# A planned two-layer decoder kernel: other durations in the planner, a time per change of TensorE's tile form, and the last sum in full width

## The chip, the core and the metric

The kernel runs on one core of one Trainium2 chip. The time is the device time of one execution in microseconds (us); lower is better. Three executions of the kernel before gave 816.85, 816.95 and 820.06 us, a median of 816.95. One execution was also recorded by the profiler; its views are what the prediction reads.

The core has five engines that run side by side, each through its own queue in order: TensorE (PE; its weight loads are PEld), VectorE (DVE), ScalarE (ACT), GpSimd (POOL) and SyncE (SP), which here only issues DMAs.

## What is computed

Two layers over 256 tokens of width 1024. Each layer mixes tokens by two attentions (nsa and moba) in parallel, merges them by gates, and then runs a gated feed-forward. In fp32 throughout:

```python
for l in range(DEPTH):                       # DEPTH = 2
    ada = jax.nn.silu(c) @ w_ada[l] + b_ada[l]
    sh_m, sc_m, g_m, sh_f, sc_f, g_f = jnp.split(ada[:, None, :], 6, axis=-1)
    h = rms_norm(x, norm_mix[l]) * (1.0 + sc_m) + sh_m
    ... = jnp.split(h @ w_in[l], split_at, axis=-1)
    y_a = nsa_mixer(...)     # compressed, selected and windowed attention
    y_b = moba_mixer(...)    # block attention
    gate_a, gate_b = jnp.split(jax.nn.sigmoid(g_br), 2, axis=-1)
    merged = gate_a * (y_a @ w_up_nsa[l]) + gate_b * (y_b @ w_up_moba[l])
    x = x + g_m * (merged @ w_out[l])
    h = rms_norm(x, norm_ffn[l]) * (1.0 + sc_f) + sh_f
    gt, up = jnp.split(h @ w_ffn_in[l], 2, axis=-1)
    x = x + g_f * ((jax.nn.silu(gt) * up) @ w_ffn_out[l])
return x
```

## The kernel before

**Tiling.** The 256 tokens are two tiles of 128 (t = 0, 1). Most weight matrices arrive in units of 128 x 2048 numbers (1 MB). A unit is split into a high part (`hi`, ScalarE, rounded to fp32r) and a low part (`lo`, VectorE, the rest), and a product is three matmuls of 512 columns: high by high, high by low, low by high (`mm3`). A few units are multiplied whole in fp32 instead (`raw`), where a matmul shows as two instructions of the trace. The split activations are called `hp` (the normalised input of a sublayer), `mT` (the merged attention) and `aT` (the feed-forward's inner tile); `yy` holds the attention outputs, which are multiplied whole.

**Stages of a run.** First a lead: constants, the first input and the first eight weight units. Then for each layer the attention (projections, score bursts `bank<-kk,qq`, softmax, value bursts `bank<-pt,vsw` and `bank<-pt,ve`, in which matmuls use 64 rows or 64 columns of the array), the up projections (`yy`), the output projection (`mT`), the joint to the feed-forward (residual sum, norm, transposes, scale and shift in `h_chain_`), the feed-forward in two halves, and a joint to the next layer.

**The planner.** The program isn't issued in the order in which it is written down. `Engines` (lines 561 to 680) records each operation as an `Op` with a duration for every engine that may run it, its predecessors, and the buffers it takes. `Program.order` (line 266) then simulates the engines with these durations: for each engine it looks at the operations that could start first, and among those within a small window (0.08 us for PE, 0.05 for DVE and ACT) takes the one of highest rank. The rank is the longest path to the end plus a boost; operations under `R.ahead()` rank above others on every engine but PE. `free[e]` is the time from which an engine may take its next operation, `ends` the time at which a result is there, and `LAT` what another engine waits beyond it. Where several engines may run an operation, the one that ends first takes it, with a handicap (`BIAS`). If PE would stand idle for long, `fill` puts dummy matmuls there (`bank<-zb`).

`Program.rounds` (line 532) makes 60 such plans. Each is replayed 8 times by `replay` (line 480) with its order held and random pauses in the DMAs; operations on chains that left PE waiting get a higher boost in the next plan. The plan whose replays ended soonest on average is emitted. The order of each engine's queue, of SP's too, is thus fixed ahead of the run; buffer waits and data waits are semaphores.

**Tile forms before.** An `Op` has a flag `parts`, true when a matmul uses fewer than 128 rows or columns. Only `replay` charges 0.1 us (`SWITCH[2]`) when the flag changes; `order` charges nothing.

**The last sum.** In the last layer's output product (line 1647 on) the four accumulators are (t, c), c being a half of the 1024 columns. For the last one, (1, 1), the last three weight units are added in two halves of 256 columns, each with its own residual sum (`resid`, line 1635) and output DMA:

```python
            parts[(NT - 1, 1)] = [(0, 256), (256, 512)]
            keys += [(i, t, k, c, e) for t in range(NT) for c in range(2) for e in parts[(t, c)]
                     for i in range(nu - nl, nu) for k in range(2)]
```

Of the kernel before, what the change touches and what calls it, by code (L numbers as in the profile page):

```python
# [107 lines left out]
def AP(x):  # L108
    return x.ap() if isinstance(x, Ref) else x
# [9 lines left out]
class Op:  # L119
    def __init__(self, no, alts, key):  # L120
# [5 lines left out]
        self.func, self.loads, self.parts, self.paced, self.then = None, None, False, False, None  # L126
# [5 lines left out]
FIRST = 1000.0  # L132
LAT = {"PE": 0.24, "DVE": 0.09, "ACT": 0.09, "POOL": 0.2, "SP": 0.0, "Q": 0.0}
# [5 lines left out]
class Program:  # L139
# [9 lines left out]
    SWITCH = (0.0, 0.0, 0.1)  # L149
# [116 lines left out]
    def order(self):  # L266
# [24 lines left out]
        parts = False  # L291
# [43 lines left out]
        while left:  # L335
# [6 lines left out]
            for op in ready:  # L342
# [15 lines left out]
            for e, cs in per.items():  # L358
# [3 lines left out]
                else:  # L362
                    w = eps[e] + (self.SWITCH[1] if e == "PE" else 0.0)
                    pick = max((c for c in cs if c[0] <= t0 + w), key=lambda c: (c[1].rank(e), -c[1].no))
# [38 lines left out]
            if e == "PE":  # L403
                parts = op.parts
# [14 lines left out]
            else:  # L419
                free[e] = t + c  # L420
# [21 lines left out]

    def fill(self, t0, t1):
# [15 lines left out]
        op.stage = "fill"  # L459
# [20 lines left out]
    def replay(self, steps, seed):  # L480
# [4 lines left out]
        dma, table, parts, gaps = 0.0, (), False, []  # L485
        for i, (e, op, c, deps) in enumerate(steps):
# [22 lines left out]
            free[e] = t + c  # L509
# [49 lines left out]
class Engines:  # L559
# [25 lines left out]
    def stt(self, out, a, s, b, op0, op1, accum=None):  # L585
# [5 lines left out]
                  [a, s, b], [out] + list(kw.values()), extra=0.08 if kw else 0.0)  # L591

    def ttr(self, out, a, b, op0, op1, init, accum):
        self._vec(("DVE",), cols(out), True,
                  lambda v: v.tensor_tensor_reduce(AP(out), AP(a), AP(b), 1.0, init, op0, op1, AP(accum)),  # L595
                  [a, b], [out, accum], extra=0.08)

    def ts(self, out, a, s1, s2, op0, op1=None, engs=("DVE",)):
# [3 lines left out]
                  [a, s1, s2], [out], psum=self._psum(a))  # L602
# [12 lines left out]
    def act(self, out, a, func, scale=None, bias=None, accum=None, late=()):  # L615
# [27 lines left out]
    def mm(self, out, lhsT, rhs, start, stop, cost=None):  # L643
# [6 lines left out]
        op.parts = AP(lhsT).shape[0] < P or AP(out).shape[0] < P  # L650

    def term(self, out, lhsT, rhs, first):
# [13 lines left out]
        self.p.op({"PE": (cost, [go])}, [lhsT, rhs], [out], term=s)  # L666

    def tr(self, out, a, ident):
        self.p.op({"PE": (0.109, [lambda: self.nc.tensor.transpose(AP(out), AP(a), AP(ident))])}, [a, ident], [out])  # L669
# [16 lines left out]

HALVED = 1
# [15 lines left out]
def trunk_kernel(tc, pools, A):  # L703
# [510 lines left out]
    def sublayer_mix(l, h):  # L1214
# [4 lines left out]
        ev, kv_, qv, vv, yv = (R.val(x_) for x_ in ("e", "kk", "qq", "ve", "yy"))  # L1219
# [7 lines left out]
        def whole_piece(d, src):  # L1227
            evac(d, src)
            return [(None, None, d[:, j * P:(j + 1) * P]) for j in range(4)]
# [571 lines left out]
```

## Time and profile before

| | us |
|---|---|
| median of three executions | 816.95 |
| the three executions | 816.85, 816.95, 820.06 |
| span of the profiled execution (first to last instruction) | 815.4 |

The executions shown are at least 1.45 us longer than the profiled span: the time around the first and the last instruction is not in the span.

How to read the lines that follow in the prediction. A line of the first view gives an engine's busy time, its share of the span and its instructions; in a line by stage, the bounds of the stage come first, then its length, the busy time of PE with the number of its instructions, the granted clock, the share of the DMA engines and GB/s. In a timeline a line starts with the time of start and the duration of the group (both in us), engine, line of the kernel, operation, result<-operands by the program's names, rows*columns for matmuls, the shape, and the number of instructions merged; in brackets stands how long the engine was idle before and what released it. In a list by form, two numbers after the bar are the busy time and the mean duration in ns. A line of one source line gives the least, the median and the greatest duration in ns. In the chain a line is start, length and what it was. L662 is the line of matmuls into shared sums, L648 that of other matmuls, L669 of transposes, L583 of VectorE's two-operand operations, L631 of ScalarE's.

### The profile page before, as it was taken

The page shows a single profiled execution, that of the slowest core. Times are in us where ns is not written, and L with a number is a line of the kernel's source. Part 1 is how long each engine was busy: PE and PEld are TensorE (multiplying, and loading weights), DVE is VectorE, ACT ScalarE, POOL GpSimd, SP SyncE. Part 2 cuts the span into 40 slices and gives each one's busy share as a digit, 9 for nine tenths or more (in the row PEclk, how much of TensorE's full clock was granted, in tenths as well). Part 3 has the DMA queues.
Part 4 walks back from the last instruction along what each step waited for, and adds up shares of the span by engine and source line. Part 5 has one row for each costly group of instructions (what it writes and reads, how often), then busy time and mean ns, then how long its engine had stood idle before and what let it go on. Part 6 is the DMA issues. An engine that isn't in the chain of part 4 may idle for free.

```text
span 815.4 us, 10543 instructions
## 1 busy us (share of the span) xinstructions
PE 803.8 (99%) x3997; PEld 610.0 (75%) x3997; DVE 580.2 (71%) x1025; ACT 410.3 (50%) x654; POOL 79.5 (10%) x75
## 2 busy tenths in 40 slices
PE   8999999999999999999999999999999999999997
PEld 4567656764878888888878887676477888889886
DVE  6889977677986877777788898776377526545454
ACT  5445366662673534433585566587347524433441
POOL 4702620000100000000000442000000000000000
PEclk9999999999999999999999999999999999999999
DMA  9967585538949887977855785540391645555441
GB/s 357 416 230 290 161 295 182 175 130 310 372 152 338 311 305 288 327 293 259 311 174 214 278 289 180 188 151 25 104 344 69 210 153 174 202 192 207 151 158 52
DMA packets 74018, 183.82 MB, mean 225 GB/s; under 512 B 4304, under 2 KB 9696, under 8 KB 73456
## 3 DMA queue, kind: packets, MB, share of 16 engines
q1 hardware_dynamic: 73920, 183.08, 63.0%
q8 instruction: 31, 0.51, 0.2%
q14 instruction: 19, 0.16, 0.1%
q0 software_dynamic: 48, 0.08, 0.0%
HBM read 182.10 MB, written 1.05 MB: 225 GB/s over the span
## 4 chain that ended last, share of the span: by engine, by line
PE 88%; DVE 4%; DMA 2%; ACT 2%; POOL 2%; issue 1%; SPq 0%; DVEq 0%; POOLq 0%
PE bank L662 77%; PE bank L648 6%; PE bank L669 5%; DMA rows<-in_rows 1%; DVE tmp L583 1%; DMA raw<-in_w_out 1%; DVE lo L583 1%; POOL tmp L601 1%; DVE tmp L601 1%; ACT hp L631 1%; ACT hi L631 1%; SPq L678 0%; POOL tmp L583 0%; POOL at L1431 0%; DVE e L583 0%
## 5 line engine op out<-in xcount | busy, mean ns | idle before, releaser
L662 PE MATMUL bank<-hi,hp 128*128 128x512 f32 (+2 forms) x1296 | 359.2, 384 | 2.2 <-DVE hp L583 1.5
L583 DVE TENSOR_TENSOR lo<-raw,hi 128x2048 fp32r<-128x2048 f32 (+2 forms) x107 | 240.4, 2261 | 104.7 <-ACT hi L631 103.8
L631 ACT ACTIVATE hi<-raw 128x2048 fp32r<-128x2048 f32 (+2 forms) x107 | 200.6, 1891 | 223.1 <-PE bank L662 181.9
L662 PEld LDWEIGHTS bank<-hi,hp 128*128 128x128 f32 x1296 | 234.1, 188 | 59.1 <-issue 7.0
L662 PE MATMUL bank<-lo,hp 128*128 128x512 f32 (+2 forms) x648 | 208.2, 383 | 0.3 <-DVE lo L583 0.2
L662 PEld LDWEIGHTS bank<-lo,hp 128*128 128x128 f32 x648 | 119.3, 188 | 24.1 <-issue 2.6
L589 DVE SCALAR_TENSOR_TENSOR aw<-aw,crow 128x1024 f32<-128x1024 f32 x80 | 96.2, 1220 | 7.5 <-DMA aw<-in_w_ada 7.3
L662 PE MATMUL bank<-hi,aT 128*128 128x512 f32 (+1 forms) x364 | 100.7, 387 | 0.0
L662 PEld LDWEIGHTS bank<-hi,aT 128*128 128x128 f32 x364 | 66.6, 188 | 13.5 <-ACT hi L631 1.0
L662 PE MATMUL bank<-raw,yy 128*128 128x512 f32 x128 | 58.7, 596 | 0.7 <-ACT yy L640 0.7
L662 PE MATMUL bank<-lo,aT 128*128 128x512 f32 (+1 forms) x182 | 58.0, 385 | 0.0
L662 PE MATMUL bank<-raw,hd 128*128 128x512 f32 (+1 forms) x112 | 49.6, 568 | 0.9 <-ACT hd L631 0.9
L662 PEld LDWEIGHTS bank<-raw,yy 128*128 128x128 f32 x128 | 23.0, 190 | 23.7 <-issue 21.8
L662 PE MATMUL bank<-hi,mT 128*128 128x512 f32 x128 | 39.9, 403 | 0.1
L662 PEld LDWEIGHTS bank<-lo,aT 128*128 128x128 f32 x182 | 34.1, 188 | 6.1
L669 PE MATMUL bank<-ident,tmp 128*128 128x128 f32 x256 | 37.5, 274 | 1.2 <-DVE tmp L985 0.7
L631 ACT ACTIVATE at<-at,nb,rqa 128x128 f32<-128x128 f32 (+1 forms) x64 | 34.2, 536 | 7.5 <-DVE nb L589 7.5
L669 PEld LDWEIGHTS bank<-ident,tmp 128*128 128x128 f32 x256 | 30.4, 140 | 9.8 <-issue 1.8
L595 DVE CUSTOM_DVE_ANT_0 at<-bank,maskf 128x128 f32<-128x128 f32 (+1 forms) x96 | 29.5, 352 | 11.3 <-PE bank L669 8.9
L662 PEld LDWEIGHTS bank<-raw,hd 128*128 128x128 f32 x112 | 20.6, 189 | 17.2 <-issue 13.4
L583 DVE TENSOR_TENSOR tmp<-tmp,bank 128x512 f32<-128x512 f32 (+1 forms) x24 | 15.1, 639 | 22.0 <-PE bank L662 21.5
L631 ACT ACTIVATE tmp<-bank 128x512 f32<-128x512 f32 (+2 forms) x43 | 20.7, 509 | 16.3 <-PE bank L662 7.0
(185 smaller groups left out, 731.3 us busy)
## 6 DMA issues: line engine op xcount, KB each, us to landing
raw<-in_w_ffn_in SPq DMA_DIRECT2D x44, 1024.0 KB, 6.3
aw<-in_w_ada SPq DMA_DIRECT2D x80, 512.0 KB, 5.7
raw<-in_w_in SPq DMA_DIRECT2D x30, 1024.0 KB, 5.2
raw<-in_w_ffn_out SPq DMA_DIRECT2D x22, 1024.0 KB, 4.9
raw<-in_w_out SPq DMA_DIRECT2D x8, 1024.0 KB, 6.2
raw<-in_w_in SPq DMA_DIRECT2D x8, 908.0 KB, 9.1
sa<-in_w_ada SPq DMA_DIRECT2D x7, 1024.0 KB, 11.9
raw<-in_w_up_nsa SPq DMA_DIRECT2D x4, 1024.0 KB, 6.2
```

Source lines behind the costliest of these rows:

```text
L583: self._vec(engs, cols(out), True, lambda v: v.tensor_tensor(AP(out), AP(a), AP(b), op=op), [a, b], [out])
L589: lambda v: v.scalar_tensor_tensor(AP(out), AP(a), AP(s), AP(b), op0=op0, op1=op1, **{k: AP(x) for k, x in kw.items()}),
L595: lambda v: v.tensor_tensor_reduce(AP(out), AP(a), AP(b), 1.0, init, op0, op1, AP(accum)),
L601: lambda v: v.tensor_scalar(AP(out), AP(a), AP(s1), AP(s2), op0=op0, **kw),
L631: op = self.p.op({"ACT": (c, [lambda: self.nc.scalar.activation(AP(out), AP(a), func, **{k: AP(x) for k, x in kw.items()})])}, reads + lis ...
L648: op = self.p.op({"PE": (cost, [lambda: self.nc.tensor.matmul(AP(out), AP(lhsT), AP(rhs), start=start, stop=stop)])}, [lhsT, rhs], [out])
L662: self.nc.tensor.matmul(AP(out), AP(lhsT), AP(rhs), start=first, stop=v.gone == v.terms)
L669: self.p.op({"PE": (0.109, [lambda: self.nc.tensor.transpose(AP(out), AP(a), AP(ident))])}, [a, ident], [out])
```

## The change

The planner's tables and prices are altered, and the last sum is written in another way. No other computation changes; the emitted order is whatever the planner makes of the new prices.

1. **Engines fall free earlier.** In `order` and `replay`, `free[e]` becomes the end less `OVER[e]`: 0.08 us for DVE, 0.1 for ACT. The end that others wait for stays.
2. **Durations.** An accumulating `stt` and `ttr` lose 0.08 us; `ts` from PSUM with a pointer scale gains 0.12; `act` with an accumulator loses 0.1; the ACT alternative of the softmax scaling costs `nh * (0.19 + nk / 1200) + 0.1` where it cost `nh * (0.295 + nk / 1200)`.
3. **Tile forms.** The flag `parts` becomes `forms`: rows and columns of the first and the last matmul of an `Op`, each rounded up to 32, 64 or 128. Transposes and sums have a form too. A change costs `turn(a, b)` = 0.15 us, and 0.05 more into a form of fewer than 128 rows and all 128 columns. `order` adds it to the start on PE after the operation was chosen, `replay` to the time at which PE is free. `STICK`, a bonus for the form that is set, and `SLACK`, a wider window, exist and are 0.
4. **The last sum** is added in full width (512 columns) to the end. The residual sum and the output DMA of (1, 1) stay in two halves of 256, and each now waits for the whole sum.
5. **`UPS_WHOLE`** names a choice for the up projections, with both layers set to what they do today; `y_pieces` takes the place of `whole_piece`.

```diff
+OVER = {"PE": 0.0, "DVE": 0.08, "ACT": 0.1, "POOL": 0.0, "SP": 0.0, "Q": 0.0}
...
-    SWITCH = (0.0, 0.0, 0.1)
+    TURN, SLACK, TALL = 0.15, 0.0, 0.05
+    FLAT, STICK = (P, P), 0.0
...
-                    if e == "PE" and op.parts != parts:
-                        est = max(est, free[e] + self.SWITCH[0])
...
-            if e == "PE":
-                parts = op.parts
+            if e == "PE" and op.forms:
+                if op.forms[0] != form:
+                    t = max(t, free[e] + self.turn(form, op.forms[0]))
+                form = op.forms[1]
...
-                free[e] = t + c
+                free[e] = t + c - OVER[e]
                 end = t + c
...
+    def turn(self, a, b):
+        return self.TURN + (self.TALL if b[0] < P <= b[1] else 0.0)
...
-                if op.stage != "fill" and op.parts != parts:
-                    parts = op.parts
-                    idle += self.SWITCH[2]
+                if op.forms and op.forms[0] != form:
+                    idle += self.turn(form, op.forms[0])
+                if op.forms:
+                    form = op.forms[1]
...
-                  [a, s, b], [out] + list(kw.values()), extra=0.08 if kw else 0.0)
+                  [a, s, b], [out] + list(kw.values()))
...
-                  [a, s1, s2], [out], psum=self._psum(a))
+                  [a, s1, s2], [out], psum=self._psum(a),
+                  extra=0.12 if self._psum(a) and isinstance(s1, Ref) else 0.0)
...
-            c += 0.2
+            c += 0.1
...
+    def formed(op, k, m):
+        f = tuple(next(w for w in (32, 64, P) if n <= w) for n in (k, m))
+        op.forms = (op.forms[0] if op.forms else f, f)
...
-            alts["ACT"] = (nh * (0.295 + nk / 1200),
+            alts["ACT"] = (nh * (0.19 + nk / 1200) + 0.1,
...
-            tt(r, b.of(e0)[:, e0:e1] if e1 - e0 < 512 else b, g[:, cs_], ALU.mult)
+            tt(r, b[:, e0:e1], g[:, cs_], ALU.mult)
...
-            keys += [(i, t, k, c, e) for t in range(NT) for c in range(2) for e in parts[(t, c)]
-                     for i in range(nu - nl, nu) for k in range(2)]
+            keys += [(i, t, k, c) for t in range(NT) for c in range(2) for i in range(nu - nl, nu) for k in range(2)]
...
-            R.boost = 20.0 * (4 - 2 * t - c) - e0 / 50 if l == L - 1 and i >= nu - nl else 0.0
-            mm3(b, aT[t][kk], us[i].hi[:, k, cs_], us[i].lo[:, k, cs_], kk == 0)
+            R.boost = 20.0 * (4 - 2 * t - c) if l == L - 1 and i >= nu - nl else 0.0
+            mm3(bs[(t, c)], aT[t][kk], us[i].hi[:, k, cs_], us[i].lo[:, k, cs_], kk == 0)
```

More of the change, by code (lines that the diff above doesn't have):

```diff
@@ L125, in __init__ @@
         self.stage, self.first, self.boost = None, False, 0.0
-        self.func, self.loads, self.parts, self.paced, self.then = None, None, False, False, None
+        self.func, self.loads, self.forms, self.paced, self.then = None, None, None, False, None
     def rank(self, e):
@@ L290, in order @@
         table = ()
-        parts = False
+        form = self.FLAT
         parked, aside = {}, set()
@@ L362, in order @@
                 else:
-                    w = eps[e] + (self.SWITCH[1] if e == "PE" else 0.0)
-                    pick = max((c for c in cs if c[0] <= t0 + w), key=lambda c: (c[1].rank(e), -c[1].no))
+                    w = eps[e] + (self.SLACK if e == "PE" else 0.0)
+                    if e == "PE" and self.STICK:
+                        pick = max((c for c in cs if c[0] <= t0 + w), key=lambda c: (
+                            c[1].rank(e) + (self.STICK if c[1].forms and c[1].forms[0] == form else 0.0), -c[1].no))
+                    else:
+                        pick = max((c for c in cs if c[0] <= t0 + w), key=lambda c: (c[1].rank(e), -c[1].no))
                     if pick[3] > 1.0 and e != "PE":
@@ L458, in fill @@
             start=True, stop=True)] * n)}, 0.0)
-        op.stage = "fill"
+        op.stage, op.forms = "fill", (self.FLAT, self.FLAT)
         return t0, op
@@ L484, in replay @@
         start, end, by = [], [], []
-        dma, table, parts, gaps = 0.0, (), False, []
+        dma, table, form, gaps = 0.0, (), self.FLAT, []
         for i, (e, op, c, deps) in enumerate(steps):
@@ L508, in replay @@
             by.append(who)
-            free[e] = t + c
+            free[e] = t + c - OVER[e]
             if e == "SP":
@@ L595, in ttr @@
                   lambda v: v.tensor_tensor_reduce(AP(out), AP(a), AP(b), 1.0, init, op0, op1, AP(accum)),
-                  [a, b], [out, accum], extra=0.08)
+                  [a, b], [out, accum])
     def ts(self, out, a, s1, s2, op0, op1=None, engs=("DVE",)):
@@ L665, in term @@
         cost = (4 * n / 2400 + 0.006) if full else n / 2400 + 0.0135
-        self.p.op({"PE": (cost, [go])}, [lhsT, rhs], [out], term=s)
+        self.formed(self.p.op({"PE": (cost, [go])}, [lhsT, rhs], [out], term=s), P, P)
     def tr(self, out, a, ident):
-        self.p.op({"PE": (0.109, [lambda: self.nc.tensor.transpose(AP(out), AP(a), AP(ident))])}, [a, ident], [out])
+        op = self.p.op({"PE": (0.109, [lambda: self.nc.tensor.transpose(AP(out), AP(a), AP(ident))])}, [a, ident], [out])
+        self.formed(op, AP(a).shape[0], P)
     def dma(self, out, src, q="SP", least=60000):
@@ L684 @@
 WHOLE_UNITS = {(0, c, 1) for c in (2328, 2840, 3352)}
+UPS_WHOLE = (True, True)
 HALVED = 1
@@ L1218, in sublayer_mix @@
         qbT, vb, rqb = {}, {}, {}
-        ev, kv_, qv, vv, yv = (R.val(x_) for x_ in ("e", "kk", "qq", "ve", "yy"))
+        ev, kv_, qv, vv = (R.val(x_) for x_ in ("e", "kk", "qq", "ve"))
+        yv = R.val("yy", dt=None if UPS_WHOLE[l] else F32R)
         E = [quarter(ev, i, i) for i in range(2)]
@@ L1225, in win, with y_pieces @@
             return load_unit(W[kh * 512:(kh + 1) * 512, c0:c0 + n], 4, n, (l, c0, kh) in WHOLE_UNITS, spare)
-        def whole_piece(d, src):
-            evac(d, src)
-            return [(None, None, d[:, j * P:(j + 1) * P]) for j in range(4)]
+        yl = None if UPS_WHOLE[l] else R.val("yy", dt=F32R)
+        def y_pieces(i, src):
+            d = quarter(yv, i, i)
+            if yl is None:
+                evac(d, src)
+                return [(None, None, d[:, j * P:(j + 1) * P]) for j in range(4)]
+            return split_into(d, quarter(yl, i, i), src)
         def heads_T(d, src):
@@ L1518, in nsa @@
                     mm(y[:, p * P:(p + 1) * P], vbd[p % 2], pcT[:, (p // 2) * P:(p // 2 + 1) * P], False, p == 3)
-            yaT[t] = whole_piece(quarter(yv, t, t), y)
+            yaT[t] = y_pieces(t, y)
         def moba(t):
@@ L1552, in moba @@
             R.key = BOOST["moba"][t]
-            ybT[t] = whole_piece(quarter(yv, 2 + t, 2 + t), y)
+            ybT[t] = y_pieces(2 + t, y)
             R.key = 0.0
@@ L1605, in sublayer_mix @@
             for w, ys in (("w_up_nsa", yaT), ("w_up_moba", ybT)):
-                u = load_unit(A[w][l][:, cs_], 4, 512, True)
+                u = load_unit(A[w][l][:, cs_], 4, 512, UPS_WHOLE[l])
                 for t in range(NT):
```

18 lines of the change are left out of this document (7 added, 11 removed).

## The prediction

> **What bounds the kernel now.** I read the page first: the engines' shares, the granted clock, the chain.
>
> ```profile
> span 815.4 us, 10543 instructions
> PE 803.8 (99%) x3997; PEld 610.0 (75%) x3997; DVE 580.2 (71%) x1025; ACT 410.3 (50%) x654; POOL 79.5 (10%) x75
> PEclk9999999999999999999999999999999999999999
> PE 88%; DVE 4%; DMA 2%; ACT 2%; POOL 2%; issue 1%; SPq 0%; DVEq 0%; POOLq 0%
> ```
>
> TensorE is busy for 803.8 of 815.4 us, at full granted clock, and 88% of the chain is its own work. A new order can win only where TensorE idles, or where its work itself is dearer for standing in that order. Second, the busy time by stage (length, then TensorE's busy time and instructions):
>
> ```profile
> 0.00:12.00 12.00, 10.33 (x47) 1.00 0.82 315
> 12.00:68.00 56.00, 54.12 (x259) 1.00 0.83 318
> 68.00:185.00 117.00, 116.54 (x609) 1.00 0.60 208
> 185.00:237.00 52.00, 50.86 (x207) 1.00 0.78 283
> 237.00:417.00 180.00, 180.00 (x865) 1.00 0.82 295
> 417.00:431.00 14.00, 13.61 (x69) 1.00 0.67 227
> 490.00:578.00 88.00, 87.61 (x515) 1.00 0.37 126
> 578.00:632.00 54.00, 52.81 (x218) 1.00 0.55 195
> 632.00:802.00 170.00, 170.00 (x819) 1.00 0.50 173
> 802.00:815.40 13.40, 8.88 (x58) 0.98 0.22 78
> ```
>
> Length less busy time is idle time: 1.67 us before 12 us, 4.52 us in the last stage, and between them 1.88 (lead), 0.46 and 0.39 (attention of the two layers), 1.14, 0.39 and 1.19 (the joints between sublayers). The two feed-forward stretches, 350 us, have none. What a plan can take out is 1.88+0.46+1.14+0.39+0.39+1.19 = **5.45 us of idle time**, and one filler that stands for planned idleness:
>
> ```profile
> 61.01 1.03 PE L456 MATMUL bank<-zb 128*128 128x512 bf16 x4
> 61.87 0.22 PE L648 MATMUL bank<-zb,identb 128*128 128x128 bf16 x1
> ```
>
> That is 0.86 us more. Third, the largest wait of a joint, from the timeline (VectorE, then the matmul that waited):
>
> ```profile
> 229.31 0.41 DVE L601 TENSOR_SCALAR tmp<-bank,mod_f 128x128 f32<-128x128 f32 x1
> 229.64 1.28 DVE L583 TENSOR_TENSOR tmp<-bank,gbc 128x512 f32<-128x512 f32 x2
> 230.95 0.69 DVE L583 TENSOR_TENSOR x<-x,tmp 128x512 f32<-128x512 f32 x1
> 231.56 0.28 DVE L583 TENSOR_TENSOR hp<-tmp,hp 128x128 fp32r<-128x128 f32 x1
> 231.90 0.50 PE L662 MATMUL bank<-hi,hp 128*128 128x512 f32 x1 [1.06 <-DVE hp L583]
> ```
>
> The subtraction that TensorE needs (hp) stood behind three 512-wide operations of the other token tile, and TensorE idled 1.06 us. Such places are what a better plan wins and a worse one loses.
>
> **Durations.** Three prices can be held against rows.
>
> ```profile
> 93.17 1.22 DVE L589 SCALAR_TENSOR_TENSOR aw<-aw,crow 128x1024 f32<-128x1024 f32 x1
> 94.32 0.07 DVE L589 DVE_READ_ACCUMULATOR aw<-aw,crow 128x1 f32 x1
> L601 DVE TENSOR_SCALAR tmp<-bank,mod_f x16: 402/409/411, 226.1 to 632.3; 128x128 f32<-128x128 f32 x16
> L631 ACT ACTIVATE at<-at,nb,rqa 128x256 f32<-128x256 f32 x32 | 18.8, 590 | 0.6 <-DVE nb L589 0.6
> L631 ACT ACTIVATION_READ_ACCUMULATOR at<-at,nb,rqa 128x1 f32 x64 | 12.1, 189 | 0.0
> ```
>
> The dot product took 1.22 us and its successor began 1.15 us after it: the new plan says 0.155+1024/960 = 1.22 with VectorE free 0.08 sooner (1.14), the old said 1.30 for both. The scale from PSUM with pointers took 0.409; new 0.155+128/960+0.12 = 0.408, old 0.288. The exponential took 0.59, with its 0.19 read of the sum 0.78 laid end to end, less if they overlap; new 0.215+256/1200+0.16+0.1 = 0.69, old 0.79. So the new durations are nearer to the rows, and where VectorE ran 210 instructions (490 to 578) the old plan held it for up to 210 x 0.08 = 17 us too long. None of this takes an instruction away: all of it reaches the time only through the order. Its price is bounded below by all 5.45+0.86 us gone (-6.3) and above by as much again (+6.3). I take **-0.25**: the search over 60 plans is the same and was fed figures that were wrong by a tenth of a microsecond or two, while the idle time is spread over six stretches, each a chain of such operations that a plan can shift but not remove; and it can lose, too (second rival). That is the value near nothing, and both ends stay for the range.
>
> [...]
>
> **Tile-form changes.** A form is the rows x columns that a matmul uses.
>
> ```profile
> 236.94 72.59 PE bank L662 x319
> 185.53 10.03 PE L662 MATMUL bank<-raw,yy 128*128 128x512 f32 x23
> 538.45 0.61 PE L662 MATMUL bank<-hi,hp 128*128 128x512 f32 x2
> 538.99 1.13 PE L648 MATMUL bank<-kk,qq 64*128 64x512 f32 x4
> 540.05 1.09 PE L669 MATMUL bank<-ident,at 128*128 128x128 f32 x8
> 62.02 0.33 PE L648 MATMUL bank<-raw,e 128*31 128x128 f32 x1
> 578.99 0.70 PE L662 MATMUL bank<-raw,yy 128*128 128x512 f32 x1 [0.70 <-ACT yy L640]
> ```
>
> The chain has 72.59/319 = 0.2276 us for one split matmul of 512 columns. The two at 538.45 have 0.54 until the score burst begins, 0.085 more than 2 x 0.2276. The burst is four instructions, two side by side by the two halves of the rows, each pair about as long as one fp32 pass (10.03/23 = 0.436, its end included): 1.06 us until 540.05, some 0.19 more than 2 x 0.436. One way in and out costs about 0.28, **0.14 per change**. The first and the last change are at 62.02 and 578.99; counting them all in the trace gives **79**. The program has 42 bursts in small forms, so at most 84 changes, and five direct neighbours have saved one each. The old replay charged 0.1 for a change between whole and partial only; the new one 0.15, and 0.2 into a form of fewer rows and full columns, near the measured price, and `order` adds it to the clock. But it enters after the choice, and STICK and SLACK are 0: no choice prefers the form that is set. Only the search over plans can favour fewer changes. From 84 to some 65 (most value bursts joined to a score burst) the bounds are +5 x 0.14 = +0.7 and -14 x 0.14 = -2.0; I take two fewer, **-0.3**, as nothing pulls harder.
>
> **Last sum.** The tail by the timeline:
>
> ```profile
> 808.08 0.40 PE L662 MATMUL bank<-hi,aT 128*128 128x256 f32 x2
> 808.32 0.28 PE L662 MATMUL bank<-lo,aT 128*128 128x256 f32 x1
> 808.44 0.40 PE L662 MATMUL bank<-hi,aT 128*128 128x256 f32 x2
> 809.31 3.54 SPq L678 DMA_DIRECT2D out<-x  x5
> 810.92 0.76 DVE L583 TENSOR_TENSOR tmp<-bank,gbc 128x256 f32<-128x256 f32 x2 [0.43 <-PE bank L662]
> 811.59 0.75 DVE L583 TENSOR_TENSOR x<-x,tmp 128x256 f32<-128x256 f32 x2
> ```
>
> Three half-width matmuls take 808.44-808.08 = 0.36, so 0.12 each; 3 units x 2 k x 3 terms x 2 halves = 36 of them are 4.32 us. In full width 18 x 0.2276 = 4.10: **-0.22**. The halves should have let the first be finished during the second, but both products start one after the other at 810.92, behind the last matmul: that cover is not used today, and nothing is lost with it. The four VectorE operations and five output transfers stay; SP's queue has nothing behind them. The smaller edits: UPS_WHOLE is true for both layers, so `y_pieces` issues what `whole_piece` did; the cheaper ACT price of the softmax scaling can move some of it from VectorE to ScalarE, both of them off TensorE's path; no DMA is added, and their order follows the program's numbers.
>
> [...]
>
> Sum: -0.25-0.3-0.22 = **-0.8 us** on the profiled 815.4. The runs shown lie 1.5 us above that span (median 816.95, 816.85 to 820.06), and I let what lies around it stand: **816.1 us**.
>
> **Rivals.** *First, the plan really improves.* Half of the 6.3 us of idle time and filler goes (3.2), changes fall by 12 (1.7), the last sum brings 0.2: -5.1, **811.8**. For it: rows and new prices agree, and the 0.288 for the 0.409 operation misled exactly the joints. Against: the chain has steps which no order shortens, such as this one:
>
> ```profile
> 196.02 7.23 DMA raw<-in_w_out
> ```
>
> TensorE arriving sooner meets the transfer instead, and 350 us have nothing to win.
>
> *Second, slower, by the early release itself.* VectorE's place in the plan falls free 0.08 before its result is there, but the choice looks only 0.05 ahead. An operation that needs the result of the one just placed therefore always loses to one that is ready, whatever its rank and boost. In the joint shown, hp depends on the scale before it; the four 512-wide residual operations, about 0.6 each, do not. Three joints with all four ahead of the last hp: 3 x 2.4 = 7.2, of which at most the 1.14+0.39+1.19 = 2.7 of the joints is paid today: +4.5, and with the 0.2 of the last sum **+4.3, 821.2**. It decides from the point where TensorE's other matmuls in the joint cover less than one such operation, 0.6 us. Against: the joints have such matmuls, and operations from two engines end at other moments; also the replay would see the gap.
>
> *Third, the overlap is no general fact,* only that of some pairs. Then the new plan runs VectorE ahead of the chip by up to 17 us in an attention stretch where it has 24 us free; at 3 us paid in each layer **822**. The successor that begins at 94.32, 0.07 before the end, speaks against it.
>
> Also the plan may come out much as it was; that is within the forecast.
>
> **Numbers.** Half a percent, 4.1 us, is about what a measurement here can tell from no change. Forecast (within it, 813.2 to 819.8 by its own): 0.58. First rival 0.21, second 0.19, third 0.02. Faster 0.21, same 0.58, slower 0.21. The range leaves out a tenth at each side, half of either rival: **811.2 to 821.3**.
>
> **What would show it.** Last sum: no 256-column matmul of hi,aT in the last layer's output, and from the last matmul to the end of the span about 4.6 us as now. Changes: a count between 74 and 82, if the forecast holds. Idle time: between 12 and 802 us four to seven microseconds; under 3 is the first rival. Second rival: hp behind 512-wide operations in more joints, with TensorE waiting for VectorE hp in total for over 5 us where it is 1.5 now. What makes all of it wrong: idle time in the feed-forward stretches, where I expect none, or a lead stage that ends at another time by over 2 us.

## The result and the profile after

Five executions of the changed kernel took 824.63 to 826.61 us, median **826.04**; five of the kernel before, beside them, a median of 817.88 (816.85 to 824.0). The ratio is **1.009**, 95% interval 1.0064 to 1.0116: slower, and outside the predicted range. The profiled execution has a span of 823.6 us, 8.2 more than before's 815.4. The page of after, shares and chain:

```profile
span 823.6 us, 10504 instructions
PE 806.7 (98%) x3976; PEld 609.4 (74%) x3976; DVE 572.6 (70%) x1016; ACT 417.9 (51%) x679; POOL 70.5 (9%) x70
...
PE 77%; DVE 8%; DMA 5%; ACT 4%; POOL 3%; issue 1%; SPq 0%; DVEq 0%; ACTq 0%; POOLq 0%
```

21 fewer matmul records (18 fewer in the last sum and 3 fewer fillers), and yet TensorE is busy 2.9 us longer and its own work is 77% of the chain where it was 88%. The busy time between 12 and 802 us, before and then after (same columns as in the prediction: bounds, length, PE, PEld, DVE, ACT, POOL, granted clock, DMA share, GB/s):

```profile
12.00:802.00 790.00, 784.55 (x3896) 596.20 (x3895) 564.70 (x988) 402.64 (x642) 73.94 (x57) 1.00 0.64 227
```

```profile
12.00:802.00 790.00, 780.14 (x3853) 590.79 (x3854) 554.42 (x975) 406.99 (x663) 65.94 (x52) 1.00 0.64 226
```

Idle time there rose from 5.45 to 9.86 us. To see where, I laid the traces over each other: every matmul is counted at one duration for its form (0.227 us for a split one of 512 columns, and so on for the others), and the **loss** at x is how much later than in before that count reaches x. A loss is good to about half a microsecond, as it depends on the durations taken. After loses 0.4 us at 40, 4.7 at 60, 6.3 at 80, 6.6 at 100, and then stays between about 6 and 10 until 7.2 at 760. TensorE has no idle time from 40 to 53 us in either trace, so three quarters of the 8.2 us arise between 53 and 100 us of the run, in the first layer's projections and the work beside them (the planner's stages postA, post and mlp). That stretch, by the windows of before, then of after:

```profile
53.00:77.00 24.00, 23.32 (x165) 16.89 (x165) 22.35 (x45) 13.80 (x29) 6.50 (x4) 1.00 0.83 310
77.00:100.00 23.00, 23.00 (x99) 15.94 (x98) 21.19 (x49) 10.92 (x19) 15.06 (x11) 1.00 0.52 168
```

```profile
53.00:77.00 24.00, 19.72 (x141) 14.42 (x140) 21.34 (x44) 13.39 (x27) 8.18 (x6) 0.93 0.79 288
77.00:100.00 23.00, 21.54 (x98) 15.14 (x96) 20.25 (x40) 11.61 (x20) 17.99 (x11) 1.00 0.66 213
```

VectorE is busy for over 43 of 47 us in before: here it is nearly as full as TensorE. TensorE's waits there, before and then after (total, times, longest):

```profile
PE bank L648 <- DVE e L583: 0.4, 1, 0.4
```

```profile
PE bank L685 <- POOL tmp L593: 1.9, 1, 1.9
PE bank L685 <- DVE kbd_tok L611: 1.5, 1, 1.5
PE bank L659 <- DVE e L593: 1.2, 2, 0.7
PE bank L685 <- ACT e L651: 1.2, 1, 1.2
```

5.8 us where there were 0.4. The longest, in after's timeline (TensorE, then the clock of the windows around it):

```profile
66.68 2.78 PE L678 MATMUL bank<-hi,hp 128*128 128x512 f32 x11
71.38 0.72 PE L685 MATMUL bank<-ident,tmp 128*128 128x128 f32 x4 [1.92 <-POOL tmp L593]
71.79 2.87 PE L678 MATMUL bank<-lo,hp 128*128 128x512 f32 x6
74.46 1.00 PE L678 MATMUL bank<-hi,hp 128*128 128x512 f32 x2
```

```profile
70.00:72.00 2.00, 0.62 (x5) 0.63 (x6) 2.00 (x3) 0.63 (x1) 1.32 (x1) 0.96 1.04 422
72.00:74.00 2.00, 2.00 (x6) 1.55 (x6) 2.00 (x5) 1.87 (x2) 1.37 (x1) 0.50 1.02 399
```

After the wait the granted clock is 0.50, and six matmuls take 2.87 us and two 1.00. The same groups in before took 1.66 and 0.62:

```profile
68.33 1.66 PE L662 MATMUL bank<-lo,hp 128*128 128x512 f32 x6
...
70.28 0.62 PE L662 MATMUL bank<-hi,hp 128*128 128x512 f32 x2
```

That is 1.6 us more. The account: 5.8 - 0.4 of waits, 1.6 of half clock, less 0.6 for fillers that before had here and after has not: 6.4, against a loss of 6.2 from 40 to 100.

The other piece is the tail. After's last matmul starts at 817.69, 5.9 us before the end; before's at 810.60, 4.8:

```profile
817.69 0.39 PE L678 MATMUL bank<-hi,aT 128*128 128x512 f32 x1
...
817.95 1.28 DVE L593 TENSOR_TENSOR x<-x,tmp 128x512 f32<-128x512 f32 x2
819.15 0.75 DVE L593 TENSOR_TENSOR tmp<-bank,gbc 128x256 f32<-128x256 f32 x2
```

The earlier residual sums stand ahead of the last one on VectorE until 819.15: +1.1 us.

### The profile page after: what moved, and what is told of

Read it like the earlier page. It is cut to its first block, busy times and chain, and to the rows that moved or that the text cites. A ratio compares the mean times of both kernels' runs of the same rounds, so it can differ in the third digit from the quotient of the medians.

```text
span 823.6 us, 10504 instructions
## 1 busy us (share of the span) xinstructions
PE 806.7 (98%) x3976; PEld 609.4 (74%) x3976; DVE 572.6 (70%) x1016; ACT 417.9 (51%) x679; POOL 70.5 (9%) x70
## 4 chain that ended last, share of the span: by engine, by line
PE 77%; DVE 8%; DMA 5%; ACT 4%; POOL 3%; issue 1%; SPq 0%; DVEq 0%; ACTq 0%; POOLq 0%
PE bank L678 67%; PE bank L685 5%; PE bank L659 5%; DVE lo L593 3%; DMA aw<-in_w_ada 2%; DVE tmp L593 2%; DMA rows<-in_rows 1%; DMA raw<-in_w_in 1%; ACT hi L642 1%; POOL tmp L593 1%; DMA raw<-in_w_ffn_out 1%; ACT at L642 1%; DVE aw L599 1%; POOL tmp L611 1%; DVE e L593 1%
## 5 line engine op out<-in xcount | busy, mean ns | idle before, releaser
L678 PE MATMUL bank<-hi,hp 128*128 128x512 f32 (+2 forms) x1296 | 363.1, 384 | 1.7 <-DVE hp L593 1.3
L678 PE MATMUL bank<-lo,hp 128*128 128x512 f32 (+2 forms) x648 | 213.6, 387 | 0.4 <-DVE lo L593 0.4
L678 PE MATMUL bank<-hi,aT 128*128 128x512 f32 x352 | 101.2, 395 | 0.3 <-ACT aT L642 0.3
L678 PEld LDWEIGHTS bank<-hi,aT 128*128 128x128 f32 x352 | 64.9, 188 | 13.9 <-ACT hi L642 0.6
L678 PE MATMUL bank<-lo,aT 128*128 128x512 f32 x176 | 57.5, 393 | 0.2 <-DVE lo L593 0.2
L678 PE MATMUL bank<-raw,yy 128*128 128x512 f32 x128 | 56.3, 594 | 0.0
L599 DVE SCALAR_TENSOR_TENSOR tmp<-tg,bank 128x512 f32<-128x512 f32 x16 | 10.7, 685 | 31.7 <-PE bank L678 31.7
L966 POOL TENSOR_TENSOR r<-r,mhalf 128x4 f32<-128x4 f32 x4 | 4.1, 1029 | 320.7 <-DVE r L611 320.6
```

What stands on the lines that cost most here:

```text
L599: lambda v: v.scalar_tensor_tensor(AP(out), AP(a), AP(s), AP(b), op0=op0, op1=op1, **{k: AP(x) for k, x in kw.items()}),
L678: self.nc.tensor.matmul(AP(out), AP(lhsT), AP(rhs), start=first, stop=v.gone == v.terms)
L966: E_.raw("POOL", 1.1 + 0.13 * n, lambda: nc.gpsimd.tensor_tensor(AP(r), AP(r), AP(mh), op=ALU.pow), [r, mhalf], [r])
```

## What GpSimd and VectorE do to each other

Both kernels give one 512-wide addition of this stretch to GpSimd. Before, then after:

```profile
72.74 2.28 DVE L583 TENSOR_TENSOR lo<-raw,hi 128x2048 fp32r<-128x2048 f32 x1
...
73.67 2.49 POOL L583 TENSOR_TENSOR tmp<-tmp,tmp 128x512 f32<-128x512 f32 x1
...
74.94 1.28 DVE L601 TENSOR_SCALAR h<-h 128x60 f32<-128x60 f32 x1
```

```profile
67.92 2.28 DVE L593 TENSOR_TENSOR lo<-raw,hi 128x2048 fp32r<-128x2048 f32 x1
68.15 3.17 POOL L593 TENSOR_TENSOR tmp<-tmp,tmp 128x512 f32<-128x512 f32 x1 [7.75 <-ACT tmp L642]
...
70.12 1.75 DVE L593 TENSOR_TENSOR tmp<-e,ct 128x512 f32<-128x512 f32 x1
71.79 0.68 DVE L593 TENSOR_TENSOR tmp<-e,st 128x512 f32<-128x512 f32 x1
```

The addition is 2.49 long here and 3.17 there, but it ends 1.14 after the end of VectorE's `lo` (76.16 less 75.02), and 1.12 (71.32 less 70.20). So by these rows it is held until `lo` is done and then takes some 1.1. VectorE's next operations are held in turn: the 128x60 scale, 0.18 in after, takes 1.28 and ends 0.06 after the addition; `tmp<-e,ct` takes 1.75 where its neighbour takes 0.68. Over the whole of both traces, the six such additions that start beside a VectorE operation with both inputs in SBUF (the split `lo`) take 2.49 to 3.28 and end 1.12 to 1.16 after it; the one that runs beside products with one input in PSUM (`e<-bank,vecs`) took 1.29. Of the two held on VectorE, `tmp<-e,ct` reads two tensors and the scale one; what makes the engines hold each other, no trace here shows.

The second long wait is the same thing twice. After:

```profile
90.07 2.27 DVE L593 TENSOR_TENSOR lo<-raw,hi 128x2048 fp32r<-128x2048 f32 x1
90.43 2.92 POOL L1412 TENSOR_TENSOR rc<-rc,mhalf 64x1 f32<-64x1 f32 x1
...
93.39 1.41 DVE L611 TENSOR_SCALAR kbd_tok<-tmp,rc 32x64 f32<-32x64 f32 x1 [0.44 <-POOL rc L1412]
...
94.02 0.73 POOL L593 TENSOR_TENSOR ct<-rows,sincos 128x256 f32<-128x256 f32 x1
...
95.88 0.24 DVE L611 TENSOR_SCALAR kbd_tok<-tmp,rc 32x64 f32<-32x64 f32 x1
```

The power `rc` ends 1.01 after `lo`; then `kbd_tok`, 0.24 alone, takes 1.41 and ends at 94.80 with GpSimd's table products (94.75). Neither plan knows of any of this: each holds the addition for 1.88 us (0.5 + 512 x 0.0027), the power for 1.2, and VectorE's operation beside them for its normal time. Two of the four waits above, 3.4 of 5.8 us, and the half clock stand behind such blocks.

The third wait, 1.2 us for `e`, has in part another reason. The plan lets the next operation start 0.08 us before the end of the one ahead on VectorE. After:

```profile
59.81 1.73 DVE L593 TENSOR_TENSOR e<-bank,vecs 64x256 f32<-64x256 f32 x4
62.12 1.73 DVE L593 TENSOR_TENSOR e<-bank,vecs 64x256 f32<-64x256 f32 x4
63.02 0.43 PE L659 MATMUL bank<-raw,e 128*31 128x128 f32 x2 [0.75 <-DVE e L593]
L593 DVE TENSOR_TENSOR e<-bank,vecs x8: 405/422/428, 59.8 to 63.4; 64x256 f32<-64x256 f32 x8
```

Four of these take 1.73 us from the first start to the last end, more than 4 x 0.422 = 1.69: none starts before the one ahead has ended, although none waits for a result. The old prices say 1.69 for four in a row, the new ones 1.69 - 3 x 0.08 = 1.45: twice 0.28 too little, about half of this wait. Of the VectorE operations between 53 and 100 us in after, 50 do start 0.07 to 0.09 before the end of the one ahead, and ten start 0.01 to 0.03 after it with nothing to wait for, six of them within these two groups. So the overlap that the early release counts on holds for most pairs, not for all; why not for `e`, whose products alternate between the two halves of the partitions, no run shows.

## The experiments

Theories named in the expectations: **A**, a term of the change itself makes worse plans (A1: the second rival, a release 0.08 early against a window of 0.05; A2: the price for changes of form; A3: the other durations). **B** or **draw**: the search keeps the best of 60 plans judged with random pauses, and the new prices just drew a worse one. **C**: the old, too long durations paid for time that the plan leaves out, and correct ones uncover it. Ratios are to the kernel before in runs beside each other, with 95% interval; loss and end of span are in us, from one profiled execution each (that of a_add_rope was 2.8 us shorter than its median, so its last column is too low).

| kernel | ratio | loss at 80 | at 100 | end of span |
|---|---|---|---|---|
| b_last | 1.0001 [0.9992, 1.0010] | -0.5 | -0.6 | 0.0 |
| b_last_seed100 | 1.0026 [1.0016, 1.0035] | -0.8 | -0.9 | +2.4 |
| b_last_seed200 | 1.0044 [1.0028, 1.0061] | 0.8 | 0.4 | +5.5 |
| only_turn | 1.0006 [0.9996, 1.0016] | -0.1 | -0.7 | +1.0 |
| only_turn_pool | 0.9998 [0.9987, 1.0008] | -1.8 | -2.7 | -0.1 |
| only_over | 1.0038 [1.0026, 1.0050] | 3.8 | 3.2 | +3.4 |
| only_dur | 1.0038 [1.0024, 1.0051] | 2.5 | 2.6 | +4.3 |
| after | 1.0090 [1.0064, 1.0116] | 6.3 | 6.6 | +8.2 |
| a_seed100 | 1.0121 [1.0103, 1.0139] | 5.2 | 5.5 | +10.9 |
| a_seed200 | 1.0047 [1.0028, 1.0066] | 3.1 | 3.8 | +4.4 |
| a_eps | 1.0087 [1.0070, 1.0105] | 5.1 | 5.4 | +9.1 |
| a_add_dve | 1.0067 [1.0052, 1.0082] | 4.3 | 4.7 | +5.0 |
| a_add_rope | 1.0104 [1.0087, 1.0121] | 5.1 | 5.4 | +6.2 |
| a_pool | 1.0077 [1.0061, 1.0093] | 3.1 | 3.4 | +8.4 |
| a_cushion | 1.0047 [1.0030, 1.0063] | 0.3 | 1.8 | +4.0 |
| a_cushion_seed100 | 1.0066 [1.0047, 1.0085] | 1.2 | 1.1 | +6.6 |
| a_cushion_seed200 | 1.0040 [1.0024, 1.0055] | 1.3 | 2.0 | +3.1 |
| a_cushion_pool | 1.0034 [1.0023, 1.0046] | 0.3 | 1.6 | +4.2 |
| a_pad_else | 1.0098 [1.0079, 1.0117] | 7.2 | 6.7 | +9.7 |

### The last sum alone, and other draws of the search

**b_last** is the kernel before with part 4 of the change only; it is the base of the other kernels with old prices.

```diff
-            keys += [(i, t, k, c, e) for t in range(NT) for c in range(2) for e in parts[(t, c)]
-                     for i in range(nu - nl, nu) for k in range(2)]
+            keys += [(i, t, k, c) for t in range(NT) for c in range(2) for i in range(nu - nl, nu) for k in range(2)]
```

> The kernel before with the last sum in full width alone; old prices. Theory A (the new prices make the plan worse): as before, ratio 0.997 to 1.003, with 18 matmuls of 512 columns for 36 of 256. Theory B (the plan is a draw among plans, and any edit draws anew): anywhere from 0.995 to 1.012, with the excess over before in a stretch that the last sum doesn't touch, since the search lands on another plan.

No change, 1.0001. In its trace the last matmul starts at 810.47 where it was 810.60, and the four VectorE operations follow 0.01 sooner than before:

```profile
810.47 0.39 PE L662 MATMUL bank<-hi,aT 128*128 128x512 f32 x1
```

```profile
810.91 0.75 DVE L583 TENSOR_TENSOR tmp<-bank,gbc 128x256 f32<-128x256 f32 x2
811.58 0.75 DVE L583 TENSOR_TENSOR x<-x,tmp 128x256 f32<-128x256 f32 x2
```

The tail's +1.1 thus belongs to after's order, not to the full width. The four others begin the random numbers of the replays elsewhere, two with old prices on b_last, two on after:

```diff
-        rng = random.Random(seed)
+        rng = random.Random(seed + 100)
```

> As b_last, with other random pauses in the replays (seeds raised by 100): the same prices and the same computation, another plan. A: within 2 us of b_last. B: 3 us or more from it, either way, the difference sitting in one or two stretches of the attention.

> The kernel before with the full-width last sum and the replay's random numbers begun 200 further: a third draw with the old prices, beside 1.0001 and 1.0026. If the new prices lose through the stretch of the first layer (theory C), the loss at 60 to 100 us of work is within 0.8 us of zero, as in the two others, and the ratio 0.999 to 1.004. If the search scatters as widely with the old prices (theory draw), it loses 2 to 6 us there in some draw and the ratio is 1.004 to 1.012.

> The changed kernel, with other random pauses in the replays (seeds raised by 100). A: ratio to before 1.007 to 1.011, as the changed kernel, and the loss again between 53 and 98 us. B: 0.998 to 1.012, and the losses of 4.3 us (53 to 77 us) and 1.6 us (85 to 98 us) not there, or others in their place.

> The changed kernel with seeds raised by 200. As for a_seed100: A 1.007 to 1.011 with the same loss in the same stretch, B 0.998 to 1.012 with losses elsewhere or none.

The draw matters, and more than I expected: 0.4% among three plans with old prices, 0.7% among three with the new. Over the whole run the best of the new (1.0047) meets the worst of the old (1.0044), and the means are 1.0024 and 1.0086. In the stretch they stay apart: at 80 us -0.8 to 0.8 with the old prices, 3.1 to 6.3 with the new. So part of after's 0.9% is its draw (and before's luck with its own), but the stretch is not.

### One part of the new prices at a time

On b_last, in this order: only the early release (**only_over**), only the price of a change of form (**only_turn**), only the durations (**only_dur**, the ScalarE price of the softmax scaling with them).

```diff
-                free[e] = t + c
+                free[e] = t + c - OVER[e]
...
-            free[e] = t + c
+            free[e] = t + c - OVER[e]
```

```diff
+                if op.forms[0] != form:
+                    t = max(t, free[e] + self.turn(form, op.forms[0]))
...
-                    idle += self.SWITCH[2]
+                if op.forms and op.forms[0] != form:
+                    idle += self.turn(form, op.forms[0])
```

```diff
-                  [a, s, b], [out] + list(kw.values()), extra=0.08 if kw else 0.0)
+                  [a, s, b], [out] + list(kw.values()))
...
+                  extra=0.12 if self._psum(a) and isinstance(s1, Ref) else 0.0)
...
-            c += 0.2
+            c += 0.1
```

> b_last with OVER (0.08 on VectorE, 0.1 on ScalarE) alone; durations and form price as before. Theory A1 (the early release makes the loss, because an operation that needs the one just placed always falls outside the 0.05 window): ratio to before 1.004 to 1.010, the loss between 53 and 125 us. A2 (the form price makes it) and A3 (the other durations make it): 0.998 to 1.003. B (a draw): anything from 0.997 to 1.010, the loss at another place.

> b_last with the price for changes of form alone (0.15 and 0.2 in the order and the replay); OVER 0 and the old durations. A2: 1.004 to 1.010 with the loss between 53 and 125 us. A1 and A3: 0.998 to 1.003. B: anything from 0.997 to 1.010.

> b_last with the other durations alone (accumulators, the scale from PSUM, the softmax scaling on ScalarE). A3: 1.004 to 1.010 with the loss between 53 and 125 us. A1 and A2: 0.998 to 1.003. B: anything from 0.997 to 1.010.

A2 falls: the price of a change of form does nothing measurable (1.0006; 80 changes against 79). The early release and the durations give 1.0038 each, where A1 and A3 allowed the other at most 1.003, so neither is the whole. One plan at 1.0038 is still within the draws with old prices (up to 1.0044); it is the stretch that tells, 3.8 and 2.5 at 80, where the five plans with old prices in the table have -1.8 to 0.8.

Both parts shorten what the plan holds VectorE and ScalarE for, but not alike. The release takes 0.08 us off every VectorE instruction, 7.5 us for the 94 that before runs between 53 and 100. The new durations touch few there: six of before's accumulating operations start in the stretch, 0.5 us of price together, and 20 ahead of it; the dearer scale from PSUM first starts at 226.1. So the release is a term large enough for the loss, and how the durations alone lose 2.5 us there, by a lead planned shorter or by their draw, stays open. Next, A1, by a choice window wider than the release:

```diff
-        eps = {"PE": 0.08, "DVE": 0.05, "ACT": 0.05, "POOL": 0.05, "SP": 0.0, "Q": 0.0}
+        eps = {"PE": 0.08, "DVE": 0.13, "ACT": 0.15, "POOL": 0.05, "SP": 0.0, "Q": 0.0}
```

> The changed kernel with the choice's window widened by what OVER takes away: 0.13 us on VectorE and 0.15 on ScalarE for 0.05, so that an operation that needs the one just placed is weighed by its rank again. A1: the loss between 53 and 125 us falls from 5 to 8 us to under 2, ratio 0.998 to 1.004. A2, A3: it stays, 1.005 to 1.012. B: anything.

1.0087 against 1.009, and 5.1 at 80 where A1 had under 2: A1 falls. An operation that needs the one just placed can now win, and nothing is better.

### GpSimd's blocks

**a_add_dve** takes the plan of after and gives the one 512-wide addition to VectorE at its place in the order:

```diff
+            if op.no == 352:
+                e = "DVE"
```

**a_add_rope** does this too and puts six table products behind the power `rc` (392) in GpSimd's queue; **a_pool** corrects GpSimd's two prices on after and plans anew:

```diff
+        late = {2377, 2378, 2379, 2380, 2381, 2382}
...
+            if op.no in late and not seen:
+                keep.append((t, e, op))
+                continue
+            plan.append((t, e, op))
+            if op.no == 392:
+                seen = True
+                plan += keep
```

```diff
-                alts[e] = (0.5 + n * (2.7e-3 if two else 2.0e-3) + extra, [lambda: fn(self.nc.gpsimd)])
+                alts[e] = (0.5 + n * (4.9e-3 if two else 2.0e-3) + extra, [lambda: fn(self.nc.gpsimd)])
...
-            E_.raw("POOL", 1.2, lambda: nc.gpsimd.tensor_tensor(AP(r)[:64], AP(r)[:64], AP(mhalf)[:64], op=ALU.pow),
+            E_.raw("POOL", 2.0, lambda: nc.gpsimd.tensor_tensor(AP(r)[:64], AP(r)[:64], AP(mhalf)[:64], op=ALU.pow),
```

> The changed kernel's own order, with one instruction moved: the 512-wide add of the rotated queries that the plan gave to GpSimd (68.15 us, 3.17 us long, priced at 1.88) goes to VectorE's queue at its place. Theory C (the new plan has lost the padding that paid for what its prices leave out, GpSimd's real durations first): TensorE's wait of 1.92 us and the half clock after it (some 1.7 us) go, time falls by 2.5 to 4 us, ratio to before 1.004 to 1.007. If the add only hides another wait: under 1 us less, 1.008 or more.

> As a_add_dve, and GpSimd's table products for layer 1 (six operations, needed only after 425 us) come after the reciprocal root rc in its queue instead of before. C: TensorE's wait of 1.46 us for kbd_tok at 96 us goes too, another 1 to 2 us less than a_add_dve. If the queue isn't what holds rc: no difference to a_add_dve beyond 0.5 us.

> The changed kernel with GpSimd's two-operand operations priced by the trace (0.5 + 4.9 ns per element in place of 2.7, and 2.0 us for rc in place of 1.2). C, GpSimd's price being the larger part of what is left out: the loss up to 100 us of work falls by 2 us or more, ratio 1.002 to 1.006. If VectorE's own slow operations beside GpSimd are the larger part: little change, 1.007 to 1.011.

The single addition seems worth about a quarter of the loss, 1.0090 to 1.0067, but the two intervals overlap, and a_add_rope, which has the same edit, gives 1.0104. The trace of a_add_dve says more:

```profile
71.01 0.63 PE L688 MATMUL bank<-ident,tmp 128*128 128x128 f32 x4 [1.52 <-DVE tmp L596]
71.39 1.63 PE L681 MATMUL bank<-lo,hp 128*128 128x512 f32 x6
```

The wait shrinks only from 1.92 to 1.52, where it was expected to go, as VectorE has to do the addition; but the six matmuls take 1.63 again, at full clock.

a_add_rope was a miss both ways: `rc` stayed 3.1 long, so the order in GpSimd's queue wasn't what held it (by the rows above it was VectorE's `lo`), and the kernel is 2.5 us slower than a_add_dve (medians 826.20 and 823.69). Its trace shows what the move did. The six products now come right behind `rc`, beside the VectorE operations that TensorE waits for:

```profile
91.20 1.02 DVE L625 TENSOR_SCALAR kbd_tok<-tmp,rc 32x64 f32<-32x64 f32 x1 [0.45 <-POOL rc L1426]
92.14 0.99 DVE L625 TENSOR_SCALAR rkb<-ss 128x8 f32<-128x8 f32 x1
```

With the `tmp` product behind them (0.70) these three take 2.7 us, where in a_add_dve they take 1.41, 0.15 and 0.21, 1.8. TensorE's wait for `kbd_tok` grows from 1.5 to 2.2, and the loss at 100 from 4.7 to 5.4. Here the rest of the order is the same, so a longer block did become a longer wait.

And a longer mean price, a_pool, has 3.1 at 80 and gives the rest back later (1.0077); as a_seed200 has 3.1 without it, this may be the draw alone. A block depends on what the other engine is doing (a 512-wide addition took 1.29 us beside the `e` products and 2.49 to 3.28 beside `lo`), so I doubt that a single price per operation can be right.

### Padding put back, and put elsewhere

**a_cushion** is after with 0.08 us more on VectorE and 0.1 on ScalarE for every instruction of the stages postA, post and mlp, in the plan only; **a_pad_else** has the same in every stage but these (`not in`); the two others of the family begin the random numbers elsewhere.

```diff
-                free[e] = t + c - OVER[e]
-                end = t + c
+                pad = self.pad(e, op)
+                free[e] = t + c - OVER[e] + pad
+                end = t + c + pad
...
+    def pad(e, op):
+        near = op.stage[1:] in ("postA", "post", "mlp")
+        return {"DVE": 0.08, "ACT": 0.1}.get(e, 0.0) if near else 0.0
...
+            c += self.pad(e, op)
```

> The changed kernel with 0.08 us (VectorE) and 0.1 us (ScalarE) added to the price of each operation of the stages between the lead and the first score bursts (postA, post, mlp of each layer) alone. C: the loss between 53 and 100 us of work falls to under 2.5 us from 6.6, ratio 1.000 to 1.005. B (a draw): no relation, 1.005 to 1.012 with the loss in the same stretch.

> The kernel after with padding in the stages postA, post and mlp, and the replay's random numbers begun 100 further. Theory C: the loss at 60 to 80 us of work stays under 1.5 us as in the first padded draw (0.5 and 0.3), where the same numbers without padding gave 2.6 and 5.2; ratio 1.002 to 1.007 (without padding 1.0121). Theory draw: 2 to 6 us at 80, ratio 1.004 to 1.012.

> As the last, begun 200 further. Theory C: the loss at 60 to 80 us of work under 1.5 us, where the same numbers without padding gave 1.1 and 3.1; ratio 1.001 to 1.006 (without padding 1.0047). Theory draw: 1 to 4 us at 80, ratio 1.003 to 1.008.

> The kernel after with the same padding (0.08 us on VectorE, 0.1 on ScalarE per instruction) in the plan of every stage but the three that were padded before (postA, post, mlp). If the padding helped because it stands for time that the plan leaves out in just those stages (theory C), the loss at 60 to 100 us of work stays, 4 to 7 us, the rest of the run may gain 0 to 2, and the ratio is 1.006 to 1.010. If any disturbance of the search does as well (theory draw), or if padding anywhere helps, the loss at 100 falls under 3 us and the ratio to 1.001 to 1.005, as with the padded three stages (1.0047).

The padded plan's windows and waits, then those of the control:

```profile
53.00:77.00 24.00, 22.61 (x164) 16.59 (x163) 21.43 (x46) 12.84 (x27) 5.64 (x6) 1.00 0.85 307
77.00:100.00 23.00, 22.44 (x91) 14.75 (x89) 20.13 (x35) 11.04 (x19) 16.89 (x11) 1.00 0.54 187
```

```profile
PE bank L666 <- DVE e L600: 0.8, 1, 0.8
PE bank L692 <- DVE tmp L600: 0.6, 1, 0.6
```

```profile
53.00:77.00 24.00, 20.64 (x151) 15.57 (x150) 20.70 (x47) 13.77 (x30) 6.43 (x6) 0.93 0.70 257
77.00:100.00 23.00, 21.06 (x84) 15.30 (x85) 22.26 (x37) 9.71 (x19) 17.30 (x11) 0.93 0.73 245
```

```profile
PE bank L692 <- DVE kbd_tok L618: 1.9, 1, 1.9
PE bank L666 <- DVE e L600: 1.3, 1, 1.3
...
```

The padding is as large as the early release, so in these stages an engine falls free as with the old prices, and a result comes 0.08 or 0.1 later than priced. With it the stretch comes back in all three draws (0.3, 1.2, 1.3 at 80, against 6.3, 5.2, 3.1 with the same random numbers unpadded), and in the first of them the clock stays at 1.00 and the waits are 1.4 us. Padding everything else leaves the loss at 7.2 and the clock at 0.93. That is the place theory C named; another draw doesn't explain it. What the padding stands for is not separated by it. Time of VectorE operations beyond the median of their form, a measure of the blocks, sums to 2.2 us between 53 and 100 in after, but to 2.1 in before and 2.3 in a_cushion, which lose nothing or little there. So a plan without room for the blocks pays for them, and one with room doesn't; the room may serve other omissions too, such as the `e` products. It isn't all: the padded draws lose another 2 to 5 us after 80, so their mean ratio is 1.0051 where that of the unpadded is 1.0086, not 1.

### A version that beats both

> The padded kernel with GpSimd priced from the trace too (4.9 ns for an element of a two-operand operation, 2.0 us for the power). Tries for a version that beats both: if the two omissions are separate and add, the loss at 60 to 125 us of work is under 1 us and the ratio 0.999 to 1.003; if the padding had already covered GpSimd, nothing is added and the ratio is 1.002 to 1.006.

> The kernel before with the full-width last sum, the price for changes of form (which alone gave 1.0006) and GpSimd priced from the trace; old durations for the rest. A try at a version that beats both: if GpSimd's omission costs something even where the old durations pad the plan, the ratio is 0.994 to 0.998; if the padding had covered it, 0.999 to 1.003, with a loss at 60 to 100 us of work within 0.8 us of zero either way.

**a_cushion_pool** joins the edits of a_cushion and a_pool: 1.0034, the best with the new durations and still slower than before. **only_turn_pool** joins only_turn and a_pool's prices on the old durations: 0.9998. It gains 2.7 us by 100, has well under one of them left at 140, and ends 0.1 sooner. No kernel here beats the one before by what can be measured.

## Why the prediction was wrong

**The bound** was read rightly: nothing but idle time in the plan's hands, none in the feed-forward, and this is where the loss lies (idle 9.86 for 5.45).

**The durations are the step that failed:** "I take -0.25: the search over 60 plans is the same and was fed figures that were wrong by a tenth of a microsecond or two". It took prices nearer to the rows for a plan about as good, and put the early release, 0.08 us on each of VectorE's instructions, at nothing. The prices are nearer to most rows; but the plan leaves out the blocks between VectorE and GpSimd, a microsecond or two each, and pairs without overlap, and the room that the old prices left on VectorE, so I read it, had covered such errors with one of the opposite sign. In place of -0.25, the release alone gives +3.0 us of the medians and the durations alone +2.8, one plan each, and room put back in three stages alone brings the loss at 80 from between 3.1 and 6.3 to between 0.3 and 1.3. My upper bound, +6.3 "as much again", came from no row; the span grew by 8.2, in part because a wait also cost clock (0.50 behind the one of 1.92 us).

**Changes of form:** 77 forecast, 81 found by the same count; at 0.14 each that is +0.3 for -0.3, and alone the price did nothing. Wrong in sign, and too small to matter. **Last sum:** -0.22 forecast; in b_last the last matmul starts 0.13 sooner, but VectorE's product behind it only 0.01 (810.91 for 810.92), and the span is the same. None of it reached the end; b_last also waits 0.47 us for ScalarE's `aT` at 804.23, which before does not, so the size of this term stays open. That "nothing is lost with it" held for b_last; in after the other sums come late, and the tail is 1.1 longer.

**First rival:** no. **Second rival:** its sign, and part of its size (+4.3 for the early release; only_over gives +3.0), but not its mechanism. TensorE waits 1.3 us in all for VectorE's `hp`, not over 5, and the wider window changed nothing. **Third rival:** nearer than I thought. "Only that of some pairs" is what the ten operations without overlap show, at some 0.1 us each, and "the new plan runs VectorE ahead of the chip" is what happened, 400 us earlier, though by the rows the blocks count for more there (2.2 us). I gave it 0.02 because I tested only the row of one pair, and not other kinds of pairs or what else stood beside VectorE. Rows for it were in the trace of before: an addition of 2.49 us that the plan held at 1.88, a 128x60 scale of 1.28, and the same `e` products, 1.73 for four.

**The signs I named** did their work: no 256-column matmul of `hi,aT`, 81 changes, idle above seven, and a lead that ends late (the first score burst at 77.20 where it was 72.39), which I had put down as what makes all of it wrong.

**Shown:** the stretch, its waits and half clock, that the early release alone loses there, and that room in these stages alone undoes the loss. **Shown for single places:** that a block makes TensorE wait; one was taken out (a_add_dve) and one made longer (a_add_rope). **Argued from rows:** that blocks and missing overlap are what the old prices paid for; a plan that knows of them wasn't tried. **Open:** how the new durations alone lose in a stretch in which they change six operations, and what makes plans of the same prices differ by 0.4 to 0.7%.

## What to carry to other kernels

A planner's prices are calibrated together with what its model leaves out: before you correct one, look for time in the trace that no price stands for, since the old error may be paying for it. Judge such a change over several draws of the search, and by the stretch where traces part, as one plan against one plan can be luck by half a percent. Test an overlap on every kind of pair before a plan counts on it. And where an engine is full beside TensorE, look at what holds its operations beyond their normal time, not only at mean durations.

## What was not expected of the hardware

- **A GpSimd operation can be held by VectorE without holding it in turn.** The powers over 128x8 elements in after (nanoseconds: least, median, greatest; first and last start):

```profile
L966 POOL TENSOR_TENSOR rqa<-rqa,mhalf x4: 2060/2342/3622, 72.6 to 463.3; 128x8 f32<-128x8 f32 x4
L966 POOL TENSOR_TENSOR rqb<-rqb,mhalf x4: 1689/1950/2950, 81.4 to 496.1; 128x8 f32<-128x8 f32 x4
L966 POOL TENSOR_TENSOR rkb<-rkb,mhalf x4: 1627/1840/2015, 88.8 to 494.2; 128x8 f32<-128x8 f32 x4
```

  All twelve end 1.49 to 1.52 us after the VectorE operation with two SBUF inputs beside which they start, whatever their length, yet VectorE runs unhindered during them: `tmp<-e,ct` and `tmp<-e,st` at 73.11 and 73.73 take 0.69 and 0.68 beside the power of 72.63 to 74.70. The VectorE operations shown above that take long beside GpSimd stand beside an addition or table products: 1.28 in before, 1.75 and 1.41 in after, 1.02 and 0.99 in a_add_rope. What makes the powers differ, no run shows.
- **Half clock after a short gap, but not after every one.** In after TensorE was busy 2.08 of the 4 us from 68 to 72, with a gap of 1.92 that ended at 71.38, and the clock was 0.50 for 3.4 us, from 71.84 to 75.25; in a_add_dve 2.48 of the same 4 us, a gap of 1.52, and it stayed at 1.00. But the length of the gap alone doesn't decide: in a_pad_else a gap of 1.30 ended at 65.74, with 3.18 of the 6 us from 60 to 66 busy, and the clock was 0.86 from 64 to 66 and 0.50 from 66 to 68; in a_add_rope TensorE waited 2.2 for `kbd_tok`, and it was 1.00 from 77 to 100. What decides, no run shows.
